# In the feed-forward part of a hybrid block: one sum of the down-projection on VectorE, the last pass's operands written by the up-projection, and the first two blocks' f read back

## The chip, the cores and the metric

The kernel runs on one core of a Trainium2 chip. The metric is the time of one execution in microseconds (us) of device time. PE is TensorE, DVE is VectorE, ACT is ScalarE, POOL is GpSimd, and SP is the engine that issues the DMAs.

## The reference

One layer over x of 2048 rows by 1024. Four mixers (a dilated attention, an RG-LRU, an SSD and a differential attention) read a projection of the normalised rows; their outputs are projected, normalised and added to x. Then comes the feed-forward part, which alone is touched here:

```
u = rms_norm(h, norm_ffn_pre)
f = square(relu(u @ w_ff_up))        # 2048 x 4096
h = h + rms_norm(f @ w_ff_down, norm_ffn_post)
```

## The kernel before

**Products.** Both projections are done by a scheme with seven products for a 2 by 2 block product in place of eight. Each number in a matmul is split into two float16 parts (a rounded one and a remainder), and each product takes three matmuls (`mm3`). A split is one ACT instruction (the rounded part) and one DVE instruction (the remainder). `TURN` is the order of the seven products: 0, 5, 6, 4, 1, 3, 2.

**Up-projection.** It has 32 blocks (g, cp): g = 0..15 is a pair of 128 columns of f, cp = 0, 1 a half of the rows. `up_block` runs the products into PSUM banks X, Y, Z, V, in the order X, Y, Z, V, X, Z, V. ACT applies relu and square into the two tiles `e` (f = 0 and 1), and `put` writes f to DRAM (`fD`). For all blocks but (0, 0) and (1, 0), `up_operands` makes the operands for j = 0 and 2 of the four j (128 rows each): four sums `fz` on POOL, seven splits `fs`, two writes to `fO`. `put` then writes only j = 1 and 3. The tiles of a block come from the pool `fuw` or, every other block, from `fst`; when the last of `fst` is released, the pools of the down-projection can open there.

**Down-projection.** It runs in six passes over g, in the order `QS` = 1, 2, 0, 3, 4, 5 (`PASSES`: passes 0 and 1 have two pairs g, the others three). A pass has eight blocks (cp, j), a block 42 matmuls in a pass of two pairs and 63 in one of three. `f_operands` gets a block's operands `fo`: for j = 0 and 2 one DMA from `fO`; for j = 1 and 3, and for all j of pass 0, cp 0, it reads f back (`fr`, one buffer) and makes them (four POOL sums `ft`, seven ACT and seven DVE instructions). `down_weights` does the same for the weights (`dr`, `ds`, `dw`), three pairs ahead.

`down_block` sums the products into y, which stays in SBUF: s = X copied by ACT (`ds`), s += Y on DVE; POOL adds s to y22, y21 and y12, in this order; DVE adds the later banks, y22 += Z first. In these names y11 and y12 are the two halves of one row tile of y and y21 and y22 those of another. The Z bank takes two products, 6 and 3, so product 3 waits until DVE has done y22 += Z, and that add waits for the add of s to y22. Three products (6 into Z, 4 into V, 1 into X) stand between the end of Y and the second use of Z. The first pass (1) has no add of s, and in the last pass (5) DVE does y12's. After each block of the last pass, `finish` normalises two row tiles on ACT, POOL (`fgp`, `ms_f`, `rs_f`) and DVE (`y<-y,rs_f,fh`) and writes them out.

**Order.** Every instruction goes through the class `Loom` (its helper at L562 records them, so all rows have that line). It lists the whole program's work and issues it by a greedy plan: each engine's queue is filled in the order in which the plan's costs make the pieces ready, with priorities by lane ("down" and "fin" 0, "fform", "fprep" and "uprep" 1, "up" 2). Each engine then runs its queue strictly in order.

Of the kernel before, what the change touches and what calls it, by code (L numbers as in the profile page):

```python
# [10 lines left out]
F32 = mybir.dt.float32  # L11
F16 = mybir.dt.float16
# [7 lines left out]
P = 128  # L20
# [14 lines left out]
QS = (1, 2, 0, 3, 4, 5)  # L35
# [1584 lines left out]
class Ffn:  # L1620
# [8 lines left out]
    def __init__(self, k, w_up, w_dn, post, gain, u, ev, out):  # L1629
# [8 lines left out]
        for q, (p0, p1) in enumerate(PASSES):  # L1638
            for cp in range(2):
                self.f[q, cp] = k.dram.tile([4, P, 2 * (p1 - p0), 2 * P], F32, tag=f"fD{q}{cp}", name=f"fD{q}{cp}")  # L1640
                self.o[q, cp] = k.dram.tile([2, P, p1 - p0, 7, 2, P], F16, tag=f"fO{q}{cp}", name=f"fO{q}{cp}")
        self.w, self.d, self.n, self.made = {}, {}, 0, 0
# [65 lines left out]
    def up_block(self, g, cp):  # L1708
# [15 lines left out]
        def act(src, f, ab):  # L1724
            d = e[f][:, :, ab, :]
            nc.scalar.activation(d, src.rearrange("p (j t) -> p j t", j=4), AF.Relu, scale=2.0 ** -24)
            nc.scalar.activation(d, d, AF.Square)

        def put(f):
            x = 2 * (g - PASSES[q][0]) + f  # L1730
            j = slice(1, 4, 2) if q + cp else slice(0, 4)
            nc.sync.dma_start(self.f[q, cp][j, :, x, :].rearrange("j p c -> p j c"),
                              e[f][:, j].rearrange("p j a t -> p j (a t)"))
        q = next(i for i, (p0, p1) in enumerate(PASSES) if p0 <= g < p1)
        with nc.lane("up", 2):
# [27 lines left out]
            act(add(V)[:], 0, 1)  # L1763
            put(0)
        if q + cp:
            self.up_operands(q, g - PASSES[q][0], cp, e)

    def up_operands(self, q, x, cp, e):

        k, nc = self.k, self.k.nc  # L1770
        with nc.lane("fform", 1, DVE=1.0):
            a = [e[f][:, 0:4:2, ab, :] for ab in range(2) for f in range(2)]
            z = [self.ev.tile([P, 512], F32, tag=f"at{i % 2}", name=f"fz{q}{x}{cp}{i}")[:, 0:256]
                 .rearrange("p (j t) -> p j t", j=2) for i in range(4)]
            sums(nc.gpsimd, *a, *z)
            src = dict(in_turn(*a, *z, False))
            for n in (0, 4):
                w = self.ev.tile([P, 2, 4, 2, P], F16, tag="e1", name=f"fs{q}{x}{cp}{n}")
                m = min(4, 7 - n)
                for i in range(m):  # L1780
                    split_to(nc, src[SHELF[n + i]], w[:, :, i, 0, :], w[:, :, i, 1, :])
                nc.sync.dma_start(self.o[q, cp][:, :, x, n:n + m].rearrange("j p i h t -> p j (i h t)"),
                                  w[:, :, 0:m].rearrange("p j i h t -> p j (i h t)"))
# [16 lines left out]
    def f_operands(self, q, cp, j):  # L1800
# [3 lines left out]
        with nc.lane("fprep", 1, DVE=1.0):  # L1804
            if q + cp and j % 2 == 0:
                w = k.fdr.tile([P, n, 7, 2, P], F16, tag="fo", name=f"fo{q}{cp}{j}", bufs=2)
                nc.sync.dma_start(w[:].rearrange("p n i h t -> p (n i h t)"),
                                  self.o[q, cp][j // 2].rearrange("p n i h t -> p (n i h t)"))
                return w
# [11 lines left out]
    def down_block(self, q, cp, j):  # L1821
# [17 lines left out]
        with nc.lane("down", 0):  # L1839
# [9 lines left out]
            if not first:  # L1849
                for o in (y22, y21, y12):  # L1850
                    (nc.gpsimd if not last or o is not y12 else nc.vector).tensor_tensor(o, o, s, op=ALU.add)
# [52 lines left out]
    def run(self):  # L1904
# [6 lines left out]
        for g, cp in blocks:  # L1911
            while ready < min(n, g + 2):
                self.up_weights(ready, 1)
                ready += 1
                for x in range(8) if ready == 2 else (ready + 5,) if 2 < ready < 11 else ():
                    self.down_top(x)
            self.up_block(g, cp)
        self.down_scale()
        self.y = [k.fd.tile([P, D], F32, tag=f"y{t}", name=f"y{t}") for t in range(NT)]
# [145 lines left out]
```

## Times and profile before

| | us |
|---|---|
| median of 3 runs (2623.23, 2630.83, 4965.94) | 2630.83 |
| the profiled execution | 2625.73 |
| its span | 2624.0 |
| PE busy / DVE / ACT / POOL | 2450.8 / 1843.2 / 1286.4 / 1157.3 |
| mean granted TensorE clock | 0.974 of full speed |

Times within the profile are from the span's start. The mixers, the output projection and the norm come before the up-projection's steady part. The down-projection's first matmul stands at 1960.82. Its first two passes (1 and 2) end near 2168, pass 0 fills 2168 to 2262, passes 3 and 4 run to about 2488, pass 5 ends at 2613, and 11 us of output follow.

### The profile page before, as it was taken

The numbers are of one execution on the slowest core, as the hardware profiler recorded it, in microseconds if no ns is written. First come the engines' busy times: TensorE is split into PE (matmuls) and PEld (weight loads), VectorE is DVE, ScalarE is ACT, GpSimd is POOL, SyncE is SP. The second block draws the span as 40 slices with busy tenths as digits, with TensorE's granted clock in tenths as the row PEclk, the third lists the DMA queues.
The fourth block names the chain that finished last, engine by engine and source line by source line (L and its number), as shares of the span: only waits on it lengthen the run. The fifth ranks groups of instructions, "written<-read, shape, count | busy, mean of one in ns | idle before, by whom it ended". The sixth has DMA issues, their size and how long they took to land.

```text
span 2624.0 us, 39878 instructions
## 1 busy us (share of the span) xinstructions
PE 2450.8 (93%) x14186; PEld 1297.1 (49%) x14186; DVE 1843.2 (70%) x3973; ACT 1286.4 (49%) x2705; POOL 1157.3 (44%) x1195
## 2 busy tenths in 40 slices
PE   7999999999999997997897999999998998999987
PEld 5555475666645555653444444444443443444433
DVE  6487986766788778757735776666648758747576
ACT  6377775433456667644435555555545323313222
POOL 5373331020266444534521444444325647747476
PEclk9999999999999998997998999999999999999998
DMA  6522226362351435236632443433334322323255
GB/s 189 151 71 85 84 71 191 66 179 56 79 149 56 123 108 161 86 90 204 197 113 78 143 148 132 145 103 107 117 118 161 126 71 87 118 96 113 78 174 163
DMA packets 277944, 313.90 MB, mean 120 GB/s; under 512 B 51381, under 2 KB 227957, under 8 KB 275184
## 3 DMA queue, kind: packets, MB, share of 16 engines
q1 hardware_dynamic: 277743, 311.35, 38.1%
q8 instruction: 112, 1.84, 0.3%
q14 instruction: 89, 0.72, 0.1%
HBM read 215.27 MB, written 102.83 MB: 121 GB/s over the span
## 4 chain that ended last, share of the span: by engine, by line
PE 60%; DVE 16%; POOL 7%; DMA 7%; issue 5%; ACT 3%; SPq 2%; DVEq 0%; POOLq 0%; ACTq 0%
PE mz L562 10%; PE mv L562 10%; PE mx L562 10%; PE my L562 5%; PE pt L562 5%; DVE e L562 3%; PE po L562 3%; PE as L562 2%; DVE fo L562 2%; PE pv L562 2%; PE do L562 2%; SPq L562 2%; PE dt L562 2%; POOL y L562 2%; DVE dw L562 1%
## 5 line engine op out<-in xcount | busy, mean ns | idle before, releaser
L562 PEld LDWEIGHTS <-fo 128*128 128x128 f16 x2688 | 264.9, 99 | 379.0 <-issue 63.6
L562 PEld LDWEIGHTS <-uw 128*128 128x128 f16 x2688 | 263.3, 98 | 311.7 <-issue 0.8
L562 PE MATMUL pt<-uuh,wl 128*128 128x512 f16 x640 | 243.9, 381 | 0.7 <-DVE wl L562 0.7
L562 PE MATMUL pt<-uuh,wh 128*128 128x512 f16 x640 | 244.3, 382 | 0.1
L562 PE MATMUL pt<-uul,wh 128*128 128x512 f16 x640 | 244.0, 381 | 0.0
L562 POOL TENSOR_TENSOR y<-y,ds 128x512 f32<-128x512 f32 x112 | 163.5, 1483 | 154.8 <-DVE ds L562 154.8
L562 DVE CUSTOM_DVE_ANT_0 e<-sc,strip,scf 128x512 f32<-128x512 f32 (+3 forms) x320 | 205.9, 663 | 25.3 <-PE sc L562 15.2
L562 PE MATMUL mz<-dw,fo 128*128 128x512 f16 x768 | 188.4, 389 | 34.0 <-DVE y L562 33.7
L562 ACT ACTIVATE e<-e,dmn 128x1024 f32<-128x1024 f32 (+4 forms) x192 | 171.4, 895 | 46.0 <-DVE dmn L562 43.4
L562 PE MATMUL mx<-dw,fo 128*128 128x512 f16 x768 | 183.4, 382 | 9.2 <-ACT ds L562 5.2
L562 PEld LDWEIGHTS <-wh 128*128 128x128 f16 x1280 | 123.2, 99 | 126.1 <-issue 22.3
L562 PE MATMUL mv<-dw,fo 128*128 128x512 f16 x768 | 184.4, 383 | 0.9 <-DVE y L562 0.9
L562 PE MATMUL po<-woh,mx 128*128 128x512 f16 x512 | 168.5, 393 | 10.6 <-ACT mx L562 6.3
L562 PE MATMUL mx<-u,uw 128*128 128x512 f16 x768 | 177.5, 380 | 0.0
L562 PE MATMUL mz<-u,uw 128*128 128x512 f16 x768 | 177.0, 379 | 0.0
L562 PE MATMUL mv<-u,uw 128*128 128x512 f16 x768 | 177.0, 379 | 0.0
L562 POOL TENSOR_SCALAR e<-e,dcf 128x256 f32<-128x256 f32 (+4 forms) x96 | 74.0, 770 | 160.9 <-DVE dcf L562 112.1
L562 ACT ACTIVATE ae<-ae,mt 128x256 f32<-128x256 f32 (+1 forms) x192 | 87.2, 455 | 114.3 <-DVE mt L562 100.2
L562 PEld LDWEIGHTS <-mx 128*128 128x128 f16 x768 | 76.6, 101 | 99.1 <-issue 9.5
L562 POOL TENSOR_TENSOR ur<-ur,g_ffn 128x1024 f32<-128x1024 f32 x32 | 61.3, 1922 | 134.4 <-DMA ur<-in_w_ff_up_dram 83.7
L562 PE MATMUL sc<-k,q 128*128 128x512 f16 (+3 forms) x320 | 102.4, 350 | 13.0 <-DVE dmn L562 9.3
L562 ACT ACTIVATE at<-dt 128x512 f32<-128x512 f32 (+3 forms) x160 | 80.7, 527 | 68.6 <-PE dt L562 64.4
(332 smaller groups left out, 5616.9 us busy)
## 6 DMA issues: line engine op xcount, KB each, us to landing
dr<-in_w_ff_down_dram SPq DMA_DIRECT2D x64, 512.0 KB, 3.7
fo<-fO SPq DMA_DIRECT2D x16, 1344.0 KB, 5.6
ur<-in_w_ff_up_dram SPq DMA_DIRECT2D x32, 512.0 KB, 5.2
fD<-e SPq DMA_DIRECT2D x60, 256.0 KB, 2.2
fO<-fs SPq DMA_DIRECT2D x30, 512.0 KB
wr<-in_w_in_dram SPq DMA_DIRECT2D x24, 512.0 KB
fr<-fD SPq DMA_DIRECT2D x16, 768.0 KB, 4.3
fO<-fs SPq DMA_DIRECT2D x30, 384.0 KB, 3.7
```

The costliest lines, as they stand in the source:

```text
L562: op.ins.append(fn(*[real(a) for a in args], **{n: real(a) for n, a in kw.items()}))
```

## The change

Four edits go together.

1. `down_block`: y22 += s is a DVE instruction in all passes that have it (5 passes of 8 blocks, 40 instructions from POOL to DVE). POOL keeps y21 and y12, and y21 alone in the last pass.
2. For the last pass (q = 5, g = 13 to 15) `up_operands` makes the operands of all four j: `fz` 512 columns wide in place of 256, the splits too, in four tiles of two operands in place of two of four (24 writes to `fO` in place of 12). `put` writes no f there. `f_operands` loads all eight `fo` of that pass; the four reads `fr` and the 4 x (4 POOL, 7 ACT, 7 DVE) instructions of blocks j = 1 and 3 are gone.
3. After the 5th and the 7th up-projection block (those are (2, 0) and (3, 0)), f of blocks (0, 0) and (1, 0) is read back from DRAM into tiles of `fuw` (`eb00`, `eb01`, `eb10`, `eb11`, 256 KB each), and `up_operands` makes their operands for j = 0 and 2: 2 x (4 POOL, 7 ACT, 7 DVE). In pass 0 the blocks (0, 0) and (0, 2) then load `fo`, and as many instructions are gone there.
4. `act` claims both tiles `e` of a block at its first write.

PE's instructions are the same in number. Up to the 5th block of the up-projection, at about 1478 us, the order on all engines is that of before.

```diff
@@ class Ffn, __init__
-                self.o[q, cp] = k.dram.tile([2, P, p1 - p0, 7, 2, P], F16, tag=f"fO{q}{cp}", name=f"fO{q}{cp}")
+                self.o[q, cp] = k.dram.tile([4, P, p1 - p0, 7, 2, P], F16, tag=f"fO{q}{cp}", name=f"fO{q}{cp}")
...
@@ up_block
             d = e[f][:, :, ab, :]
+            nc.claim(e[0], e[1])
...
-            nc.sync.dma_start(self.f[q, cp][j, :, x, :].rearrange("j p c -> p j c"),
-                              e[f][:, j].rearrange("p j a t -> p j (a t)"))
+            if q != QS[-1]:
+                nc.sync.dma_start(self.f[q, cp][j, :, x, :].rearrange("j p c -> p j c"),
+                                  e[f][:, j].rearrange("p j a t -> p j (a t)"))
...
+        self.made_last = e
         if q + cp:
             self.up_operands(q, g - PASSES[q][0], cp, e)
@@ up_operands
         with nc.lane("fform", 1, DVE=1.0):
-            a = [e[f][:, 0:4:2, ab, :] for ab in range(2) for f in range(2)]
-            z = [self.ev.tile([P, 512], F32, tag=f"at{i % 2}", name=f"fz{q}{x}{cp}{i}")[:, 0:256]
-                 .rearrange("p (j t) -> p j t", j=2) for i in range(4)]
+            js = slice(0, 4, 1 if q == QS[-1] else 2)
+            nj, ni = (4, 2) if q == QS[-1] else (2, 4)
+            if e is None:
+                e = [k.fuw.tile([P, 4, 2, P], F32, tag="er", name=f"eb{x}{f}", bufs=2) for f in range(2)]
+                nc.claim(*e)
+                nc.need(*self.made_last.values())
+                for f in range(2):
+                    nc.sync.dma_start(e[f][:, js].rearrange("p j a t -> p j (a t)"),
+                                      self.f[q, cp][js, :, 2 * x + f, :].rearrange("j p c -> p j c"))
+            a = [e[f][:, js, ab, :] for ab in range(2) for f in range(2)]
+            z = [self.ev.tile([P, 512], F32, tag=f"at{i % 2}", name=f"fz{q}{x}{cp}{i}")[:, 0:nj * P]
+                 .rearrange("p (j t) -> p j t", j=nj) for i in range(4)]
             sums(nc.gpsimd, *a, *z)
             src = dict(in_turn(*a, *z, False))
-            for n in (0, 4):
-                w = self.ev.tile([P, 2, 4, 2, P], F16, tag="e1", name=f"fs{q}{x}{cp}{n}")
-                m = min(4, 7 - n)
+            for n in range(0, 7, ni):
+                w = self.ev.tile([P, nj, ni, 2, P], F16, tag="e1", name=f"fs{q}{x}{cp}{n}")
+                m = min(ni, 7 - n)
...
@@ f_operands
-            if q + cp and j % 2 == 0:
+            if j % 2 == 0 or q == QS[-1]:
...
@@ down_block
             if not first:
-                for o in (y22, y21, y12):
+                add(y22, y22, s)
+                for o in (y21, y12):
                     (nc.gpsimd if not last or o is not y12 else nc.vector).tensor_tensor(o, o, s, op=ALU.add)
@@ run
             self.up_block(g, cp)
+            if self.made in (5, 7):
+                self.up_operands(0, (self.made - 5) // 2, 0, None)
```

The plan lays the queues out anew from these edits. Three places show it. The first is ACT in the up-projection, at the block after the first read-back: `e21...` are the f tiles of block (2, 1), `fs10..` the split operands of block (1, 1), `fs00..` those of the block read back, `uw4_...` the seven weight operands of g = 4. Before:

```order
L562 ACTIVATE fs1004_16754<-fz1000_16708 128x2x128
L562 ACTIVATE fs1004_16754<-fz1001_16729 128x2x128
L562 ACTIVATE fs1004_16754<-fz1002_16737 128x2x128
L562 ACTIVATE e211_16770<-c21_16735 128x4x128
L562 ACTIVATE e211_16770<-e211_16770 128x4x128
L562 ACTIVATE e210_16792<-mx_16669 128x4x128
```

After the change:

```order
L562 ACTIVATE fs0004_16835<-fz0002_16815 128x2x128
L562 ACTIVATE uw4_0_16844<-ur40_16655,s_up4_16827 128x512
L562 ACTIVATE uw4_5_16847<-us41_16768,s_up4_16827 128x512
L562 ACTIVATE uw4_6_16853<-us42_16785,s_up4_16827 128x512
L562 ACTIVATE uw4_4_16856<-us40_16752,s_up4_16827 128x512
L562 ACTIVATE uw4_1_16860<-ur40_16655,s_up4_16827 128x512
L562 ACTIVATE uw4_3_16863<-ur41_16667,s_up4_16827 128x512
L562 ACTIVATE uw4_2_16866<-us43_16803,s_up4_16827 128x512
L562 ACTIVATE e211_16869<-c21_16739 128x4x128
L562 ACTIVATE e211_16869<-e211_16869 128x4x128
L562 ACTIVATE e210_16870<-mx_16669 128x4x128
L562 ACTIVATE e210_16870<-e210_16870 128x4x128
```

Ahead of this piece stand the four rounded parts `fs0000` and the first two of `fs0004`. So the seven splits of the block read back and the seven of g = 4's weights now stand between `fs1004` and `e210<-mx`, the instruction that frees bank X; before, the weights' stood behind it. On POOL the order there is `us42`, `fz0000`, `us43`, `fz0001`, `fz0002`, `fz0003`.

The second place is DVE in pass 0, block (0, 3), where `ds003` is s, y7 holds y22 and y21, y3 holds y11 and y12, and `dw9_...` are weight splits for g = 9. Before:

```order
L562 TENSOR_TENSOR ds003_22944<-ds003_22944,my_22959 128x512
L562 SCALAR_TENSOR_TENSOR dw9_6_22966<-ds92_22949,kd_14614,dw9_6_22966 128x512
L562 SCALAR_TENSOR_TENSOR dw9_4_22973<-ds90_22845,kd_14614,dw9_4_22973 128x512
L562 SCALAR_TENSOR_TENSOR dw9_1_22976<-dr91_22884,kd_14614,dw9_1_22976 128x512
L562 TENSOR_TENSOR y7_21345<-y7_21345,mz_22927 128x512
```

After the change:

```order
L562 SCALAR_TENSOR_TENSOR dw9_4_22989<-ds90_22877,kd_14614,dw9_4_22989 128x512
L562 TENSOR_TENSOR ds003_23003<-ds003_23003,my_22999 128x512
L562 TENSOR_TENSOR y7_21411<-y7_21411,ds003_23003 128x512
L562 TENSOR_TENSOR y7_21411<-y7_21411,mz_22982 128x512
L562 SCALAR_TENSOR_TENSOR dw9_1_22997<-dr91_22892,kd_14614,dw9_1_22997 128x512
```

The weight splits that stood between s and y22 += Z stand ahead of s or behind the add.

The third place is DVE in the last pass, block (0, 2): y6 holds y22 and y21, y2 holds y11 and y12, and y5 is a row tile that is being finished. Before, block (0, 0), where `fo501` is the next block's operands:

```order
L562 TENSOR_TENSOR ds500_25004<-ds500_25004,my_24999 128x512
L562 TENSOR_TENSOR fo501_24986<-fr501_24825,fo501_24986 128x3x128
L562 TENSOR_TENSOR y0_21256<-y0_21256,ds500_25004 128x512
L562 TENSOR_TENSOR fo501_24986<-ft501_24876,fo501_24986 128x3x128
L562 TENSOR_TENSOR y4_21267<-y4_21267,mz_24981 128x512
```

After the change, block (0, 2), which is the pattern of the later blocks:

```order
L562 TENSOR_TENSOR ds502_25209<-ds502_25209,my_25205 128x512
L562 SCALAR_TENSOR_TENSOR y5_21299<-y5_21299,rs_f5_25214,fh5_25133 128x1024
L562 TENSOR_TENSOR y6_21420<-y6_21420,ds502_25209 128x512
L562 TENSOR_TENSOR y2_21419<-y2_21419,ds502_25209 128x512
L562 TENSOR_TENSOR y6_21420<-y6_21420,mz_25186 128x512
```

No split of `fo` is left in the pass; a step of `finish` and the two adds of s stand between s and y22 += Z. At the passage to the down-projection, POOL's order was `fz5200`, `ds42`, `fz5201`, `fz5202`, `fz5203`, `ds43` and is now `ds42`, `fz5200`, `ds43`, `fz5201`, `fz5202`, `fz5203`, with `fz` twice as wide.

## Rows read from the trace of the kernel before

**Rows 1.** Windows: start:end, us, busy (x) by engine, PEclk, DMA share, GB/s.

```profile
1450.00:1955.00 505.00, 505.00 (x2354) 231.61 (x2353) 324.64 (x582) 282.07 (x537) 202.67 (x194) 1.00 0.36 121
1955.00:2002.00 47.00, 36.53 (x159) 15.48 (x158) 38.92 (x61) 27.36 (x58) 23.65 (x23) 0.96 0.55 190
2002.00:2168.00 166.00, 165.00 (x764) 74.50 (x762) 115.95 (x168) 55.66 (x112) 93.11 (x76) 1.00 0.32 108
2168.00:2262.00 94.00, 78.05 (x333) 33.31 (x332) 76.70 (x100) 28.71 (x61) 67.90 (x56) 0.95 0.31 99
2262.00:2502.00 240.00, 233.69 (x1075) 105.36 (x1073) 146.30 (x203) 60.23 (x115) 137.59 (x108) 0.99 0.29 100
2502.00:2613.00 111.00, 97.08 (x428) 42.26 (x426) 86.28 (x84) 27.90 (x56) 80.67 (x78) 0.97 0.56 173
```

**Rows 2.** Waits 1930 to 2624: who waited for whom, us, times, longest.

```profile
PE mz L562 <- DVE y L562: 33.7, 15, 4.0
DVE y L562 <- POOL y L562: 21.4, 16, 1.8
```

**Rows 3.** PE timeline, passes 0, 4, 5: start, us, instruction, [idle before <-releaser].

```profile
2213.30 1.97 PE L562 MATMUL mz<-dw,fo 128*128 128x512 f16 x6 [3.86 <-DVE y L562]
2411.76 3.72 PE L562 MATMUL mz<-dw,fo 128*128 128x512 f16 x9 [4.00 <-DVE y L562]
2540.89 2.10 PE L562 MATMUL mz<-dw,fo 128*128 128x512 f16 x9
2558.95 3.73 PE L562 MATMUL mz<-dw,fo 128*128 128x512 f16 x9 [3.92 <-DVE y L562]
```

**Rows 4.** DVE timeline, pass 0, block (0, 3).

```profile
2207.98 0.67 DVE L562 TENSOR_TENSOR ds<-ds,my 128x512 f32<-128x512 f32 x1
2208.58 2.41 DVE L562 SCALAR_TENSOR_TENSOR dw<-ds,kd,dw 128x512 f16<-128x512 f32 x2
...
2212.57 0.68 DVE L562 TENSOR_TENSOR y<-y,mz 128x512 f32<-128x512 f32 x1
```

**Rows 5.** POOL timeline, pass 0 block (0, 3) and pass 4.

```profile
2208.73 5.05 POOL L562 TENSOR_TENSOR y<-y,ds 128x512 f32<-128x512 f32 x3 [1.96 <-DVE ds L562]
2405.96 4.59 POOL L562 TENSOR_TENSOR y<-y,ds 128x512 f32<-128x512 f32 x3 [2.50 <-DVE ds L562]
```

**Rows 6.** Groups of tile y, 1990 to 2613: duration min/median/max ns, first, last start.

```profile
L562 POOL TENSOR_TENSOR y<-y,ds x112: 1255/1444/2925, 2061.1 to 2607.6; 128x512 f32<-128x512 f32 x112
L562 DVE SCALAR_TENSOR_TENSOR y<-y,rs_f,fh x14: 1271/1540/3354, 2503.7 to 2608.1; 128x1024 f32<-128x1024 f32 x14
```

**Rows 7.** DVE and POOL timelines of the last pass, two blocks.

```profile
2535.21 2.59 DVE L562 TENSOR_TENSOR y<-y,ds 128x512 f32<-128x512 f32 x1
2534.90 2.35 POOL L562 TENSOR_TENSOR y<-y,fgp 128x1024 f32<-128x1024 f32 x1
2601.72 0.69 DVE L562 TENSOR_TENSOR y<-y,ds 128x512 f32<-128x512 f32 x1
```

**Rows 8.** ACT, POOL and PE timelines of the up-projection, 1481 to 1500.

```profile
1484.82 1.34 ACT L562 ACTIVATE fs<-fz 128x256 f16<-128x256 f32 x4 [5.31 <-POOL fz L562]
1489.28 0.60 ACT L562 ACTIVATE e<-mx 128x512 f32<-128x512 f32 x1 [0.58 <-PE mx L562]
1495.15 1.93 ACT L562 ACTIVATE uw<-us,s_up 128x512 f16<-128x512 f32 x3
1488.81 1.45 POOL L562 TENSOR_TENSOR us<-ur,us 128x512 f32<-128x512 f32 x1
1494.48 2.75 PE L562 MATMUL mx<-u,uw 128*128 128x512 f16 x12
```

**Rows 9.** POOL, ACT and PE timelines at the passage to the down-projection.

```profile
1985.88 0.72 POOL L562 TENSOR_TENSOR fz<-e,fz 128x256 f32<-128x256 f32 x1
1988.36 0.58 ACT L562 ACTIVATE ds<-mx 128x512 f32<-128x512 f32 x1
1988.99 2.72 PE L562 MATMUL mx<-dw,fo 128*128 128x512 f16 x6 [5.24 <-ACT ds L562]
```

More of the change, by code (lines that the diff above doesn't have):

```diff
@@ L1771, in up_operands @@
         with nc.lane("fform", 1, DVE=1.0):
-            a = [e[f][:, 0:4:2, ab, :] for ab in range(2) for f in range(2)]
-            z = [self.ev.tile([P, 512], F32, tag=f"at{i % 2}", name=f"fz{q}{x}{cp}{i}")[:, 0:256]
-                 .rearrange("p (j t) -> p j t", j=2) for i in range(4)]
+            js = slice(0, 4, 1 if q == QS[-1] else 2)
[10 more added lines that the diff above has]
+                 .rearrange("p (j t) -> p j t", j=nj) for i in range(4)]
             sums(nc.gpsimd, *a, *z)
             src = dict(in_turn(*a, *z, False))
-            for n in (0, 4):
-                w = self.ev.tile([P, 2, 4, 2, P], F16, tag="e1", name=f"fs{q}{x}{cp}{n}")
-                m = min(4, 7 - n)
+            for n in range(0, 7, ni):
+                w = self.ev.tile([P, nj, ni, 2, P], F16, tag="e1", name=f"fs{q}{x}{cp}{n}")
+                m = min(ni, 7 - n)
                 for i in range(m):
                     split_to(nc, src[SHELF[n + i]], w[:, :, i, 0, :], w[:, :, i, 1, :])
-                nc.sync.dma_start(self.o[q, cp][:, :, x, n:n + m].rearrange("j p i h t -> p j (i h t)"),
+                nc.sync.dma_start(self.o[q, cp][js, :, x, n:n + m].rearrange("j p i h t -> p j (i h t)"),
                                   w[:, :, 0:m].rearrange("p j i h t -> p j (i h t)"))
@@ L1804, in f_operands @@
         with nc.lane("fprep", 1, DVE=1.0):
-            if q + cp and j % 2 == 0:
+            if j % 2 == 0 or q == QS[-1]:
                 w = k.fdr.tile([P, n, 7, 2, P], F16, tag="fo", name=f"fo{q}{cp}{j}", bufs=2)
                 nc.sync.dma_start(w[:].rearrange("p n i h t -> p (n i h t)"),
-                                  self.o[q, cp][j // 2].rearrange("p n i h t -> p (n i h t)"))
+                                  self.o[q, cp][j].rearrange("p n i h t -> p (n i h t)"))
                 return w
```

## The prediction

> **What bounds the kernel now.** I read the windows by stage first [rows 1], because an average over the span would mix stages with different limits. In the up-projection (1450 to 1955) TensorE is busy 505.00 of 505 us: nothing that another engine saves there can be worth anything, and anything that makes TensorE wait there costs its full length. The window 2002 to 2168 (passes 1 and 2) gives the pitch of a matmul: 165.00 us / 764 = 0.216 us. By that pitch the other windows lose
>
> - 1955 to 2002: 47 - 159 x 0.216 = 12.7 us,
> - 2168 to 2262 (pass 0): 94 - 333 x 0.216 = 22.1 us,
> - 2262 to 2502 (passes 3 and 4): 240 - 1075 x 0.216 = 7.8 us,
> - 2502 to 2613 (pass 5): 111 - 428 x 0.216 = 18.6 us.
>
> So the down-projection from pass 0 on loses 48.5 us in all, part of it idle and part of it at a lower granted clock (0.95 to 0.99).
>
> Next, who is waited for [rows 2]: TensorE's product into Z waits 33.7 us, 15 times, for a DVE add into y, and DVE's y in turn 21.4 us for POOL's y. The timeline of PE shows such stalls of about 4 us [rows 3]; the matmuls behind one run slower (nine in 3.73 us where nine take 2.10), so a stall of 4.0 us costs about 1.6 us more.
>
> What holds that add up is seen in one block of pass 0 [rows 4, 5]. s is ready at 2208.65. DVE then splits weights (two in 2.41 us, more behind them), while POOL adds s to y22, y21 and y12, three in 5.05 us. y22 += Z starts only at 2212.57, and TensorE goes on at 2213.30 [rows 3]. From the end of product Y, three products stand ahead of the one that needs Z free: 3 x 6 x 0.216 = 3.9 us in a pass of two pairs, 3 x 9 x 0.216 = 5.8 us in one of three. That is the due time which decides.
>
> **The change part by part.**
>
> *y22 += s on DVE.* Forty instructions leave POOL, whose three take 4.59 to 5.05 us in these rows [rows 5] (median 1.44 each [rows 6]), and DVE gets forty of 0.69 us where POOL leaves it alone, 2.59 us where not [rows 7]. The path is now s 0.67, y22 += s 0.69, y22 += Z 0.68: 2.0 us after Y, if nothing stands between. The order shows nothing between them in the block whose rows I read; where operands are split, one or two splits stay between, and two splits beside POOL take 2.41 us [rows 4], so 4.5 us against 3.9.
>
> - Pass 0: I allow 0.6 us for six of its eight blocks, 3.6 us. It gives back 22.1 - 3.6 = 18.5 us. That two of its blocks load `fo` and split nothing is in this sum. Ends: 8 us (the splits of all blocks stay ahead and POOL holds them) and 22.
> - Passes 3 and 4: the due time is 5.8 us, so 2.0 plus two splits fits. I leave 1.3 us: gain 6.5 us (ends 3 and 7.8).
>
> *Last pass.* Its splits leave POOL, ACT and DVE altogether, and that work is hidden except on DVE's way to y22 += Z. But two other things stand there now: a step of `finish` (1.27 us at the least, 1.54 median, 3.35 at the most [rows 6]) and both adds of s. Cheapest: 0.67 + 1.27 + 0.69 + 0.69 + 0.68 = 4.0 us, no stall. Dearest: 0.67 + 3.35 + 2.59 + 2.59 + 0.68 = 9.9 us, a stall of 4.1 us in every block. With the median step and one of the adds held by POOL: 0.67 + 1.54 + 2.59 + 0.69 + 0.68 = 6.2 us, 0.4 us late; I take 0.8 us per block for the differences between blocks, 6.6 us in all. Gain 18.6 - 6.6 = 12 us (ends 4 and 18). The four `fo` loads more replace four `fr` reads; the DMA share of the window is 0.56 [rows 1], and a load has a whole block of 63 x 0.216 = 13.6 us to land: nothing.
>
> *The read-back in the up-projection.* Its DMAs and POOL sums stand beside other work, yet ACT's queue does not absorb it. Before, ACT frees bank X with `e<-mx` at 1489.28 to 1489.88, and TensorE needs X at 1494.48 [rows 8]: 4.6 us to spare. Now the seven splits of the block read back and the seven of g = 4 stand ahead of it. POOL's `us43` ended at 1488.81 + 1.45 = 1490.3; the four `fz` are added ahead of the moment when the first tile can be finished, 4 x 0.72 us [rows 9], so 1493.1. From there ACT does four splits (4 x 1.34 / 4 = 1.3 us), seven weight splits (7 x 1.93 / 3 = 4.5 us) and three instructions of 0.6 us: bank X is free at 1500.7, and TensorE has waited 1500.7 - 1494.5 = 6.2 us. With the slower matmuls behind such a stall (1.6 us), 7.8 us. Since nothing waits for anything but TensorE here, all of it reaches the end. Ends: 0 (POOL takes `fz` so early that ACT is through in the 5.31 us which it now idles ahead of its splits [rows 8]) and 15 (the second read-back stalls as well). At the second, POOL's four sums stand together and the last weight splits behind `e<-mx`; what is added ahead of it is the seven splits, 7 x 0.34 = 2.3 us of a slack like the 4.6 us, so I cost it at nothing; if that slack is gone, it costs as much as the first.
>
> *Wider operands at the end of the up-projection.* `fz` over 512 columns takes POOL 1.26 us (its shortest add of that width [rows 6]) in place of 0.72 [rows 9]. For block (15, 1): 4 x 0.54 = 2.2 us later release of the tile on which the pools of the down-projection wait, so 2.2 us later loads. For block (15, 0): 2.2 us again, a `ds` of 1.26 us that is now ahead of the last three sums, and four wider ACT splits, 4 x (0.64 - 0.34) = 1.2 us [rows 8]. Behind these splits stands ACT's `ds<-mx` at 1988.36, and for it TensorE already waits 5.24 us [rows 9]. So the sum goes straight onto that wait: 2.2 + 2.2 + 1.3 + 1.2 = 6.9 us. Ends: 2.2 (only the loads) and 10. The earlier blocks of g = 13 to 15 have the 2.2 us more on POOL inside a slack like those 4.6 us and are costed at nothing.
>
> *Sum*: -18.5 - 6.5 - 12 + 7.8 + 6.9 = -22.3 us. The profiled execution took 2625.7 us; it lies between the two lower of the runs shown (2623.2 and 2630.8, the latter the median). So **2603.4, forecast 2604 us**.
>
> **A rule against the change.** Each moved add reads two tiles in SBUF, and the rows show what POOL does to it: started 0.31 us behind a POOL instruction of 2.35 us it took 2.59 us, and alone 0.69 us [rows 7]. The Trainium skill's page "SBUF — State Buffer", section "Who interferes with whom", states this as an exclusive lock: a VectorE instruction with two SBUF inputs contends with a GpSimd instruction that reads SBUF, and the second to issue blocks fully. By that rule the trace agrees, and moving an add between these two engines frees neither. If all forty moved adds took 2.59 us, the path in passes of two pairs would be 0.67 + 2.59 + 0.68 = 3.9 us, just the due time, and in those of three pairs within 5.8 us. So I keep the gain for passes 0, 3 and 4; the place where the lock decides is the last pass, which makes the fourth rival.
>
> **The rivals.**
>
> 1. *As summed*, 2604 us: chance 0.50.
> 2. *The adds come in order behind splits and steps of `finish`.* TensorE goes on waiting for the same add, now behind DVE's own queue. For it: one or two splits between s and y22 += Z in four blocks of pass 0, a step of `finish` in seven of the last pass. Against: the due times. Gains of 9, 5 and 8 in place of 37 in all: -22 + 14.7 = -7, so 2618 us. Chance 0.22.
> 3. *The costs are hidden.* The read-back's splits and the wider ones find room: for it ACT's idle 5.31 us; against it TensorE's 505.00 of 505, which leaves no room behind a stall. -37 + 2 gives 2591 us. Chance 0.16.
> 4. *Slower: the last pass locks.* Three two-input instructions stand in a row on DVE ahead of y22 += Z while POOL runs its normalising products of 2.35 us. If each of the three is held as in the dearest case, seven blocks stall 4.1 us and pay 1.6 us of clock: 40 us in place of 18.6, +21. With pass 0, 3 and 4 as summed: +21 - 25 + 14.7 = +11, so 2637 us. It decides from the point where y22 += Z ends more than 5.8 us behind Y. For it: 2.59 and 3.35 us occur. Against: they do not occur together in the rows, and POOL has four `ft` sums per odd block less. Chance 0.09.
> 5. That the change does not do what it says: the order has the forty adds on DVE, no split in the last pass, and the loads. No chance; what is left (0.03) is for a second stall in the up-projection beside the first, at about 2612 us.
>
> **How the numbers follow.** The likeliest case's own range is 2594 to 2614. The range for 8 in 10 takes in most of case 3 and case 2 with 6 us of difference between runs: 2589 to 2624. Case 4 and the best of case 3 are left out. Two per cent is 53 us, and about what a measurement of this kernel tells from no change: below 2578 us no case lies but the sum of all the upper ends (0.02), above 2683 us none but a disturbed measurement or several stalls at once (0.01). Within: 0.97.
>
> **What would show it.** Right: window of pass 0 down from 94 to about 76 us; the wait of PE's `mz` for DVE's y down from 33.7 to about 10 us; a stall of PE's `mx` of about 6 us near 1494 with ACT's `e` named; the wait for ACT's `ds` after the up-projection up from 5.2 us to about 10. Wrong: no stall near 1494 (rival 3), DVE rows `y<-y,ds` of more than 2 us in the last pass with `mz` stalls of 4 us behind them (rival 4), or splits standing between `ds` and `y<-y,mz` where PE waits (rival 2).

## The result, and the profile after

The changed kernel takes 2610.08 us (median of 6 runs, 2604.17 to 3146.88) against 2631.1 for the kernel before (6 runs). The ratio is 0.9923 with a 95% interval of 0.9903 to 0.9942, so some 20 us less; the forecast was 2604 us in a range of 2589 to 2624. The comparison leaves disturbed runs, such as the longest ones here, out; without them these medians are 2609.07 and 2630.83 us, and that of the add alone, in the table of experiments, is 2605.31 in place of 2607.08. The profiled execution took 2611.13 us (span 2609.4), 14.6 us less than the one before; between two profiled executions the unchanged part ahead of the feed-forward part alone differs by several us (the last transposes of its norm start between 1416.6 and 1429.0 in the kernels told of below), so stages are compared below by what TensorE loses in each.

Four windows of the changed kernel, with the columns of [rows 1] and cut at about the same places of the program: the up-projection, pass 0, passes 3 and 4, and the last pass.

```profile
1450.00:1955.00 505.00, 499.35 (x2326) 228.75 (x2324) 340.30 (x590) 286.60 (x542) 217.63 (x198) 1.00 0.39 130
2183.00:2260.00 77.00, 70.97 (x323) 31.42 (x322) 69.38 (x95) 23.58 (x48) 55.35 (x42) 1.00 0.36 123
2260.00:2500.00 240.00, 237.32 (x1091) 106.98 (x1090) 164.10 (x218) 60.39 (x114) 116.22 (x87) 0.99 0.29 102
2500.00:2599.00 99.00, 92.63 (x424) 41.26 (x422) 71.45 (x70) 20.09 (x36) 62.19 (x62) 1.00 0.69 216
```

The first window is no longer full: TensorE idles 5.65 us of 505. Pass 0's window fell from 94 to 77 us (some 2 us of that because it holds 323 matmuls where it held 333), the last pass's from 111 to 99. The waits from 1930 on, as in [rows 2]; the line of DVE's y for POOL's y, 21.4 us before, is not there any more:

```profile
PE mz L562 <- DVE y L562: 14.0, 17, 2.2
PE mx L562 <- ACT ds L562: 9.9, 1, 9.9
```

Its PE timeline at the stalls, which answers to [rows 3] and to the PE rows of [rows 8, 9]:

```profile
1502.87 2.75 PE L562 MATMUL mz<-u,uw 128*128 128x512 f16 x12 [1.91 <-ACT e L562]
1512.83 2.75 PE L562 MATMUL mz<-u,uw 128*128 128x512 f16 x12 [2.03 <-DVE c L562]
...
1970.02 1.46 PE L562 MATMUL mx<-dw,fo 128*128 128x512 f16 x3 [2.88 <-DMA fo<-fO]
...
2003.62 2.72 PE L562 MATMUL mx<-dw,fo 128*128 128x512 f16 x6 [9.88 <-ACT ds L562]
...
2217.40 1.46 PE L562 MATMUL mz<-dw,fo 128*128 128x512 f16 x6 [1.26 <-DVE y L562]
...
2229.14 1.45 PE L562 MATMUL mz<-dw,fo 128*128 128x512 f16 x6 [1.64 <-DVE y L562]
...
2550.30 2.10 PE L562 MATMUL mz<-dw,fo 128*128 128x512 f16 x9 [0.82 <-DVE y L562]
```

Stalls of up to 4 us for DVE's y in the down-projection have become stalls of at most 2.2 us; new ones stand in the up-projection, and the one at the passage has grown from 5.24 to 9.88 us.

In the table, a stage's loss is the sum, over the rows of PE's timeline, of the time to the next row's start less the number of matmuls times 0.216 us, where that is over 0.15 us (so idle time and slower matmuls together). The passage is the stretch from the first down-projection matmul to some 25 us behind the last of the up-projection.

| loss, us | before | after | after - before | forecast |
|---|---|---|---|---|
| up-projection | 0.0 | 6.3 | +6.3 | +7.8 |
| passage | 12.9 | 20.0 | +7.1 | +6.9 |
| passes 1 and 2, rest | 1.5 | 2.7 | +1.2 | 0 |
| pass 0 | 21.8 | 7.3 | -14.5 | -18.5 |
| passes 3 and 4 | 8.4 | 4.8 | -3.6 | -6.5 |
| pass 5 | 18.4 | 6.6 | -11.8 | -12 |
| sum | 63.0 | 47.7 | -15.3 | -22.3 |

### The profile page after: what moved, and what is told of

Its sections match the earlier page's. It is cut to its first block, busy times and chain, and to the rows that moved or that the text cites. A ratio compares the mean times of both kernels' runs of the same rounds, so it can differ in the third digit from the quotient of the medians.

```text
span 2609.4 us, 39806 instructions
## 1 busy us (share of the span) xinstructions
PE 2445.9 (94%) x14186; PEld 1296.0 (50%) x14186; DVE 1868.3 (72%) x3985; ACT 1283.8 (49%) x2677; POOL 1111.3 (43%) x1139
## 4 chain that ended last, share of the span: by engine, by line
PE 61%; DVE 16%; DMA 8%; POOL 6%; issue 5%; ACT 3%; SPq 2%; DVEq 0%; POOLq 0%; ACTq 0%
PE mz L562 10%; PE mv L562 10%; PE mx L562 10%; PE my L562 5%; PE pt L562 5%; PE po L562 4%; DVE e L562 3%; DVE y L562 2%; PE as L562 2%; PE pv L562 2%; PE do L562 2%; PE dt L562 2%; SPq L562 2%; PE ao L562 1%; PE atp L562 1%
## 5 line engine op out<-in xcount | busy, mean ns | idle before, releaser
L562 PE MATMUL mx<-dw,fo 128*128 128x512 f16 x768 | 183.7, 382 | 14.6 <-ACT ds L562 9.9
L562 PE MATMUL mz<-dw,fo 128*128 128x512 f16 x768 | 182.8, 381 | 14.0 <-DVE y L562 14.0
L562 POOL TENSOR_TENSOR y<-y,ds 128x512 f32<-128x512 f32 x72 | 113.7, 1596 | 156.9 <-DVE ds L562 156.9
```

What stands on the lines that cost most here:

```text
L562: op.ins.append(fn(*[real(a) for a in args], **{n: real(a) for n, a in kw.items()}))
```

## The experiments

**The parts alone.** The first kernel has the first edit alone:

```diff
-                for o in (y22, y21, y12):
+                add(y22, y22, s)
+                for o in (y21, y12):
```

> Only the first edit: y22 += s on DVE in all passes, nothing else. Theory (each edit acts in its own stage): passes 0, 3 and 4 get nearly what they got in the whole change (pass 0 there -14.7 us, passes 3 and 4 -3.5), the up-projection and its end are as before, and the last pass, with its splits still on DVE, gains a few us: 2608 to 2614 us against 2626, the stalls of the product into Z behind DVE's y down from 33.7 to about 16 us. Rival (pass 0 gains because two of its blocks load their operands and split nothing): pass 0 still loses over 14 of its 22 us, and the whole is above 2616.

The second has the second edit alone: `up_operands` for four j where q == QS[-1], no f written there, all eight `fo` of pass 5 loaded.

> Only the last pass's operands made in the up-projection; all adds of s but y12's in the last pass stay on POOL, nothing is read back. Theory: the end of the up-projection loses the 7 us that it lost in the whole change (wait for ACT's ds near 10 us), pass 5 gains 8 to 12 us, the other passes are as before: 2620 to 2626 us. Rival (the last pass gains because of the add on DVE, not because of its splits): pass 5 still loses over 14 us, and the whole is at 2630 or more.

The third has the read-back and the claim alone:

```diff
+            nc.claim(e[0], e[1])
...
-            if q + cp and j % 2 == 0:
+            if j % 2 == 0:
...
+            if self.made in (5, 7):
+                self.up_operands(0, (self.made - 5) // 2, 0, None)
```

> Only f of the first two blocks read back and their operands made in the up-projection (with the claim of both tiles). Theory: the up-projection loses 5 to 6 us in stalls as in the whole change, pass 0 gains 2 to 6 us of its 22 since two of its blocks split nothing: 2624 to 2630 us, no gain. Rival (pass 0's gain comes from here): pass 0 gains over 8 us, 2618 to 2623.

The fourth is the whole change less the read-back:

```diff
-            if j % 2 == 0 or q == QS[-1]:
+            if q + cp and j % 2 == 0 or q == QS[-1]:
...
-            if self.made in (5, 7):
-                self.up_operands(0, (self.made - 5) // 2, 0, None)
```

> The whole change without the read-back (the first blocks' operands are made in pass 0 as before). Theory: the 5 to 6 us of stalls in the up-projection are gone, pass 0 loses 2 to 6 us more than in the whole change: 2606 to 2611 us, about as the whole change. Rival: pass 0 falls back by 8 us or more, 2614 or more.

Measured, with the losses by stage as in the table above (us; the ratio of the whole change is that of the result, against its own six runs of the kernel before):

| | median | ratio to before (95%) | up | passage | 1, 2 | 0 | 3, 4 | 5 | sum |
|---|---|---|---|---|---|---|---|---|---|
| before | 2627.3 | | 0.0 | 12.9 | 1.5 | 21.8 | 8.4 | 18.4 | 63.0 |
| add alone | 2607.08 | 0.9922 (0.9902 to 0.9943) | 0.0 | 13.4 | 1.1 | 12.5 | 4.6 | 14.4 | 46.0 |
| last pass alone | 2624.52 | 0.9995 (0.9984 to 1.0006) | 4.3 | 19.4 | 2.9 | 23.0 | 8.6 | 5.9 | 64.0 |
| read-back alone | 2627.76 | 1.0003 (0.9989 to 1.0017) | 5.2 | 15.1 | 0.2 | 17.7 | 9.2 | 19.7 | 67.2 |
| no read-back | 2606.7 | 0.9929 (0.991 to 0.9948) | 1.3 | 18.8 | 4.0 | 12.3 | 4.5 | 6.6 | 47.4 |
| whole change | 2610.08 | 0.9923 (0.9903 to 0.9942) | 6.3 | 20.0 | 2.7 | 7.3 | 4.8 | 6.6 | 47.7 |

The theory held in its main point, that each edit acts in its own stage, and in three of four totals (the add alone came out 1 us better than its 2608); its sizes did not all hold. Pass 0 gave the add alone 9 us and not "nearly" 14.5, the waits for DVE's y fell to 21.1 us there and not to 16, and the last pass alone lost 4.3 us in the up-projection that its theory did not have. The rivals fell in all four: with the add alone pass 0 lost 12.5 us and not over 14, and without the read-back it fell back by 5 us and not by 8. What the prediction had not expected stands in the ratios: **the one line gives the whole gain**, and the other two edits give back what they cost. The last pass's operands save 12.5 us in pass 5 (18.4 to 5.9) and cost 6.5 us at the passage and 4.3 in the up-projection; the read-back saves 4 to 5 us in pass 0 and costs 5 in the up-projection.

**How the one line acts.** The prediction read [rows 2] as one chain: TensorE waits for y22 += Z, and that add for POOL's y22 += s. For most of the stalls the rows show something else. Of TensorE's 15 waits before the change (33.7 us), only four, 4.4 us together, stand behind an add for which DVE had waited for POOL; none of TensorE's waits follows the other twelve of DVE's 16 waits for POOL. In the remaining eleven, 29.3 us, DVE had no gap: between s and y22 += Z it worked through splits, and in the last pass through y12's add and a step of `finish` too. In the block of [rows 4] a third split, 1.74 us from 2210.91 on, stands ahead of the add. Another such block is (0, 0) of pass 0, before the change, DVE and then POOL:

```profile
2168.11 0.68 DVE L562 TENSOR_TENSOR ds<-ds,my 128x512 f32<-128x512 f32 x1
2168.71 0.41 DVE L562 TENSOR_TENSOR fo<-ft,fo 128x256 f16<-128x256 f32 x1
2169.04 2.89 DVE L562 TENSOR_TENSOR fo<-fr,fo 128x256 f16<-128x256 f32 x2
2171.86 1.48 DVE L562 TENSOR_TENSOR fo<-ft,fo 128x256 f16<-128x256 f32 x1
2173.26 0.67 DVE L562 TENSOR_TENSOR y<-y,mz 128x512 f32<-128x512 f32 x1
```

```profile
2168.86 4.19 POOL L562 TENSOR_TENSOR y<-y,ds 128x512 f32<-128x512 f32 x3 [2.23 <-DVE ds L562]
```

Beside POOL's adds the last three splits take 1.4 to 1.5 us each, where the first takes 0.41. The first of POOL's three adds, y22's, was done by about 2170.3 (an estimate: a third of 4.19 us), 3 us before y22 += Z started. The same block in the kernel with the add alone:

```profile
2166.31 0.68 DVE L562 TENSOR_TENSOR ds<-ds,my 128x512 f32<-128x512 f32 x1
2166.91 0.41 DVE L562 TENSOR_TENSOR fo<-ft,fo 128x256 f16<-128x256 f32 x1
2167.24 0.68 DVE L562 TENSOR_TENSOR y<-y,ds 128x512 f32<-128x512 f32 x1
2167.85 0.41 DVE L562 TENSOR_TENSOR fo<-fr,fo 128x256 f16<-128x256 f32 x1
2168.18 0.68 DVE L562 TENSOR_TENSOR y<-y,mz 128x512 f32<-128x512 f32 x1
```

Two splits stand between s and y22 += Z in place of four, none is slowed, and TensorE waits 0.71 us here where it waited 3.01. So the line acts at least in part through the order: with y22 += s in DVE's own queue, the plan puts y22 += Z close behind it and the splits elsewhere. A rival follows from this that no run tested, the add left on POOL and the splits planned behind y22 += Z. How much of the 20 us is due to the engine and how much to the order stays open.

**The last pass.** What still holds pass 5 when its operand work is gone is seen in the kernel with the second edit alone, DVE and then POOL at one block (columns as in [rows 4, 5]):

```profile
2547.81 2.93 DVE L562 SCALAR_TENSOR_TENSOR y<-y,rs_f,fh 128x1024 f32<-128x1024 f32 x1
...
2552.51 0.69 DVE L562 TENSOR_TENSOR y<-y,mz 128x512 f32<-128x512 f32 x1 [1.16 <-POOL y L562]
```

```profile
2551.13 1.35 POOL L562 TENSOR_TENSOR y<-y,ds 128x512 f32<-128x512 f32 x1
...
2552.58 1.26 POOL L562 TENSOR_TENSOR y<-y,ds 128x512 f32<-128x512 f32 x1
```

POOL's y22 += s still releases DVE here, and TensorE still loses only 0.9 us a block. Moving that add brings nothing more once that work is gone (5.9 us against 6.6 in pass 5). The other way round, the add alone leaves pass 5 at 14.4 us although no split stands between s and y22 += Z there any more: the step of `finish` takes up to 3.35 us and in three blocks starts only after a wait of 1.23 to 1.25 us for POOL. Which part of the work that the second edit removes (on POOL, ACT or DVE) had delayed that step was not taken apart.

In the whole change a block of pass 5 reads so on DVE, with POOL's normalising product beside it (second fence):

```profile
2543.76 0.69 DVE L562 TENSOR_TENSOR ds<-ds,my 128x512 f32<-128x512 f32 x1 [3.27 <-PE my L562]
2544.36 3.01 DVE L562 SCALAR_TENSOR_TENSOR y<-y,rs_f,fh 128x1024 f32<-128x1024 f32 x1
2547.30 2.35 DVE L562 TENSOR_TENSOR y<-y,ds 128x512 f32<-128x512 f32 x2
2549.57 0.68 DVE L562 TENSOR_TENSOR y<-y,mz 128x512 f32<-128x512 f32 x1
```

```profile
2543.93 2.36 POOL L562 TENSOR_TENSOR y<-y,fgp 128x1024 f32<-128x1024 f32 x1
...
2547.75 1.35 POOL L562 TENSOR_TENSOR y<-y,ds 128x512 f32<-128x512 f32 x1
```

The step of `finish` takes 3.01 us beside POOL where others take 1.28, and the add ends at 2550.25, when TensorE has been waiting 0.8 us. The next kernel plans that step later:

```diff
-        with nc.lane("fin", 0):
+        with nc.lane("fin", 0, DVE=3.0):
```

> The whole change, with the DVE step of finish planned 3 us later, so that it stands behind y22 += Z in the last pass. Theory: the 0.8 us by which each of seven blocks of pass 5 is late comes from that step (3.01 us beside POOL), so these stalls go, with about 1 us left of 6.6: 25 to 27 us below the kernel before, where the whole change is 20 below. Rival (the two adds of s alone, held by POOL, are late): the stalls stay above 0.5 us per block, 20 to 22 below.

Measured: median 2606.57, ratio 0.9915 (0.9891 to 0.994). Pass 5 loses 0.0 us, as expected; the rest is as in the whole change (43.8 us in all). The profile's line of PE's waits for DVE's y, 5.4 us in pass 5 of the whole change, is gone from that stretch, while the two adds of s still take 2.34 us together. So the step of `finish` was the cause, not the adds. The gain of 22 us against before lies at the rival's end of the total; by the profile the theory holds, and the total's interval is wider than the difference.

**The passage.** The long wait there follows the last block's operands on POOL, then ACT (whole change):

```profile
1999.11 1.27 POOL L562 TENSOR_TENSOR fz<-e,fz 128x512 f32<-128x512 f32 x1
```

```profile
2000.41 2.19 ACT L562 ACTIVATE fs<-fz 128x512 f16<-128x512 f32 x4 [7.91 <-POOL fz L562]
...
2002.98 0.58 ACT L562 ACTIVATE ds<-mx 128x512 f32<-128x512 f32 x1
```

Two kernels take the sums `fz` from POOL to DVE, first for both blocks of g = 15, then for (15, 0) alone (there on the change without the read-back and with `finish` later):

```diff
-            sums(nc.gpsimd, *a, *z)
+            sums(nc.vector if (q, x) == (5, 2) else nc.gpsimd, *a, *z)
```

> The whole change, with the four wide sums fz of the two blocks of g = 15 on DVE in place of POOL. Theory (POOL's wide sums hold the tiles on which the down-projection's pools wait): the wait for ACT's ds falls from 9.9 us to 5 or 6, the wait for the first fo from 2.9 to under 1; the passage loses 13 to 15 us in place of 20: 25 to 27 us below the kernel before. Rival (ACT's wider splits or the loads set it): the wait for ds stays above 8.5 us, 19 to 21 below.

Measured: median 2615.45, ratio 0.9946 (0.9927 to 0.9965). The wait for `ds` fell to 5.5 us, as expected, and that for the first `fo` to 1.3 (under 1 was expected), but the passage lost 23.9 us: other waits came. ACT first, then PE:

```profile
1973.93 0.63 ACT L562 ACTIVATE fs<-fz 128x512 f16<-128x512 f32 x1 [4.79 <-DMA fO<-fs]
```

```profile
1977.73 0.59 PE L562 MATMUL mx<-dw,fo 128*128 128x512 f16 x1 [4.29 <-ACT dw L562]
...
2007.53 2.72 PE L562 MATMUL mx<-dw,fo 128*128 128x512 f16 x6 [5.50 <-ACT ds L562]
```

The second edit writes four tiles `fs` per block where there were two. Once the sums are early, ACT's last split waits 4.79 us for the write to DRAM of an earlier tile, and the weight splits behind it in ACT's queue, which TensorE needs, wait with it. (Whether two tiles would have spared that wait was not tried.)

> The whole change without the read-back, with the step of finish planned later, and the four wide sums of the very last block of the up-projection, (15, 0), alone on DVE. Theory (POOL's queue holds the last sums, and in the run with both blocks' sums on DVE the new waits came from block (15, 1)'s): the wait for ACT's ds is 5 to 6 us in place of 9.9 and no new wait over 2 us comes in; pass 5 loses about 0; the whole is 28 to 34 us below the kernel before. Rival (DVE's sums delay whatever stands behind them in either block): new waits of 4 us or more at the passage, 22 to 26 below.

Measured: median 2600.95, ratio 0.9907 (0.9891 to 0.9924); losses 1.3, 18.6, 2.5, 11.9, 3.0, 0.0, in all 37.3 us, the least of all kernels here. Two waits of the run with both blocks' sums on DVE, 4.29 us for ACT's `dw` and 2.88 us for DVE's `c`, are gone, so block (15, 1)'s early sums had brought them; one of 2.47 us for `fo` (2.82 in that run) is there, and the wait for `ds` fell only to 8.66 us. DVE, then ACT and PE:

```profile
1984.29 0.69 DVE L562 TENSOR_TENSOR fz<-e,e 128x512 f32<-128x512 f32 x1 [1.36 <-ACT e L562]
1985.02 1.64 DVE L562 TENSOR_TENSOR fz<-fz,e 128x512 f32<-128x512 f32 x1
...
1988.25 1.78 DVE L562 TENSOR_TENSOR fz<-e,fz 128x512 f32<-128x512 f32 x1
```

```profile
1994.40 0.63 ACT L562 ACTIVATE fs<-fz 128x512 f16<-128x512 f32 x1 [2.66 <-DMA fO<-fs]
```

```profile
1996.05 2.72 PE L562 MATMUL mx<-dw,fo 128*128 128x512 f16 x6 [8.66 <-ACT ds L562]
```

The first sum takes 0.69 us; while POOL sums weights from 1984.52 on, the next three take 1.64 to 1.78. Then ACT waits again for a write. So neither held as written: no new wait of 4 us, but 25 us below before and not 28. DVE's four sums took 5.7 us beside POOL's work, and without ACT's wait of 2.66 us the wait for `ds` would have been 6.0 (an estimate: 8.66 less 2.66). This version is below both kernels in median, by 0.9% against the one before; against the changed one the intervals overlap.

Of the next three, the first and the last change the plan alone: the order of the queues, not what an instruction waits for on the chip. The second puts changes together.

**POOL's adds behind DVE's.**

```diff
                 for o in (y21, y12):
+                    if not last:
+                        nc.need(y[tb])
```

> The whole change, with POOL's adds of s to y21 and y12 made to start only after DVE's y22 += s (not in the last pass). Theory (POOL's adds hold DVE's): y22 += s falls from a median of 1.24 us to about 0.7, and pass 0 loses 3 to 5 us in place of 7.4: 23 to 25 us below the kernel before. Rival (splits in DVE's own queue ahead of the add decide): the add gets shorter, but pass 0 still loses over 6 us, 19 to 22 below.

Measured: median 2611.26, ratio 0.9923 (0.9902 to 0.9944); pass 0 lost 9.1 us. The median of y22 += s on DVE fell to 0.87 us, but in the block with the longest stall POOL's adds still started 0.18 us ahead of it, and it took 1.75: the plan's dependence does not bind the engines. So it does not tell what POOL's adds cost, and that stays open.

**Three together**: this one, `finish` later and both blocks' sums on DVE, on the change without the read-back.

> The whole change without the read-back, with all three: the step of finish later, the sums of g = 15 on DVE, POOL's adds behind DVE's. Theory: the parts add up, -20 for the change as it is, -6 for finish, -6 for the passage, -3 for POOL: about 35 us below the kernel before, near 2592. Rival (what one stall gives back, the next takes, since the plan is laid anew): under 28 us below.

Measured: median 2608.23, ratio 0.9921 (0.9904 to 0.9939); losses 1.4, 23.8, 2.0, 13.0, 4.6, 0.0. The rival held. Against the change without the read-back (12.3 in pass 0, 18.8 at the passage), of the 6.6 us won in pass 5, 5.0 were lost at the passage and 0.7 in pass 0.

**Splits planned later.** In pass 0 of the whole change, DVE at block (0, 3) (compare [rows 4]):

```profile
2212.12 2.62 DVE L562 SCALAR_TENSOR_TENSOR dw<-ds,kd,dw 128x512 f16<-128x512 f32 x2 [0.24 <-ACT dw L562]
2214.66 0.67 DVE L562 TENSOR_TENSOR ds<-ds,my 128x512 f32<-128x512 f32 x1
2215.37 1.19 DVE L562 TENSOR_TENSOR y<-y,ds 128x512 f32<-128x512 f32 x1
2216.66 0.69 DVE L562 TENSOR_TENSOR y<-y,mz 128x512 f32<-128x512 f32 x1
```

Now the splits stand ahead of s and make s itself late. So:

```diff
-        with nc.lane("fprep", 1, DVE=1.0):
+        with nc.lane("fprep", 1, DVE=4.0):
...
-        with nc.lane("dprep", prio, DVE=1.0):
+        with nc.lane("dprep", prio, DVE=4.0):
```

> The whole change, with the DVE parts of the operand and weight splits in the down-projection planned 4 us later, so that in pass 0 no split stands between s and y22 += Z, and fewer ahead of s. Theory (what passes 0, 3 and 4 still lose, 7.4 and 4.9 us, is DVE's own queue: splits ahead of s and of the add): pass 0 loses 2 to 4 us and passes 3 and 4 together under 2.5; 25 to 28 us below the kernel before. Rival (POOL's lock on the adds is what is left): pass 0 still loses over 6 us; or the later splits come too late for TensorE and appear as waits for dw or fo.

Measured: median 2612.31, ratio 0.9946 (0.9926 to 0.9966). Passes 3 and 4 lost 0.6 us: there the queue of splits was the cause. Pass 0 still lost 8.5, part of it a new wait of 1.8 us for `fo`; at the passage the wait for `ds` fell to 6.0 us, but waits of 3.4 us for DVE's `dw` and 2.6 for `fo` took its place, so that passage and passes 1 and 2 together lost 23.2 us where the whole change lost 22.7. That is the rival's second half. In pass 0 the splits now stand behind y22 += Z but ahead of the next add, the one out of V, for which TensorE waits 1.16 us twice; so the cause of what pass 0 loses is not settled by this run.

**The first edit with the plan changed**, `finish` later and, from pass 0 on, the operand splits 4 us later:

> Only the first edit, y22 += s on DVE, with two changes of the plan: the DVE step of finish 3 us later, and from pass 0 on the DVE parts of the operand splits 4 us later, so that hardly any split stands between s and y22 += Z. No wide operands, no read-back. Theory (the path s, y22 += s, y22 += Z is what counts, and the other two edits only pay for themselves): the passage loses 13 us as before the change, pass 0 5 to 7, passes 3 and 4 under 2, pass 5 under 3: 35 to 42 us below the kernel before, 2585 to 2592. Rival (the last pass needs its splits gone, and splits planned later come too late for TensorE): pass 5 loses over 8 us or waits for fo appear; under 25 below.

Measured: median 2613.86, ratio 0.994 (0.9923 to 0.9958); losses 0.0, 12.9, 1.4, 17.4, 7.6, 6.1. The rival held. One row of PE shows why:

```profile
2206.23 3.03 PE L562 MATMUL mx<-dw,fo 128*128 128x512 f16 x7 [5.85 <-DVE fo L562]
```

The split that was moved out of the add's way came 5.85 us too late for the next block: on DVE it ran at 2205.23, behind weight splits, although ACT's half of it was done at 2199.7.

**The same plan on the change without the read-back:**

> The same two changes of the plan on the whole change without the read-back: the last pass's operands come from the up-projection. Theory: the passage loses 20 us, 7 more than without the wide operands, and pass 5 gains 1 to 3 us less than that: 28 to 36 us below the kernel before, 4 to 7 us behind the run with the first edit alone and the same plan. Rival (with splits out of the last pass it is the better one): ahead of that run.

Measured: median 2608.69, ratio 0.9924 (0.9909 to 0.9939); losses 1.4, 19.3, 4.4, 16.9, 7.5, 0.0. The 28 us of the theory were missed by 9. Its median is ahead of the run with the first edit alone, which loses 6.1 us in pass 5; but the intervals overlap, and by the losses it is behind (49.5 us in all against 45.4), so which of the two is better is not shown.

## Why the prediction was right

**The forecast** held: 2610 us in 2589 to 2624, and the direction. In part that is luck. By the losses the change is worth 15.3 us and by the profiled executions 14.6, where the sum had 22.3; the medians differ by 21 us in part because the one of before lies 5 us above the execution from which the forecast was counted. And the mechanism was read rightly only down to y22 += Z. TensorE's second product into Z did wait for that add, and with y22 += s on DVE no wait of DVE for POOL's y is left; but 29.3 of the 33.7 us of stalls stood behind splits in DVE's own queue and not behind POOL's y22 += s. That these splits leave the gap was seen in the order of the queues, and the gain is there for that reason at least in part. Five of the steps, by their own terms:

- *Pass 5*, 12 us forecast, 11.8 measured, and 0.8 us per block as forecast. But where the sum had 0.67 + 1.54 + 2.59 + 0.69 + 0.68 the rows show 0.69 + 3.01 + 2.35 + 0.68: beside POOL it is the step of `finish` that is long, rather than one add. The moved add has no part in this gain, since without it (the last pass alone) pass 5 loses 5.9 us.
- *Passage*, 6.9 us forecast, 7.1 measured, on the wait that was named: `ds` 4.64 us longer (5.24 to 9.88) where 4.7 of the sum were for it. For the loads the sum had 2.2 us and their wait grew by 1.1 (1.75 to 2.88); 1.6 us of slower matmuls behind that wait, which were not in the sum, make up for it.
- *Read-back*, 7.8 us forecast, 4.9 measured in three stalls (1.91, 2.03 and 0.46 us idle); the rest of the 6.3 is a wait of 1.24 us for the scale of the down weights at 1908, which only kernels with the wider operands have. ACT's rows there, to set beside those of [rows 8]:

```profile
1495.53 1.33 ACT L562 ACTIVATE fs<-fz 128x256 f16<-128x256 f32 x4 [6.95 <-POOL fz L562]
...
1502.24 0.58 ACT L562 ACTIVATE e<-mx 128x512 f32<-128x512 f32 x1
```

  The bank was free at 1502.8, close to the 1500.7 worked out (the block as a whole runs 1.1 us later in this execution); the due time was wrong. TensorE needed that bank not for the next X at 1494.48 but for the Z after it, two products of 2.59 us later, as the row at 1502.87 says (`mz`, not `mx`). And the splits made DVE late as well (the stall at 1512.83), which I had not costed.
- *Pass 0*, 18.5 us forecast, 14.5 measured; *passes 3 and 4*, 6.5 and 3.6. **This is the term that was mis-sized**: I left 3.6 us to pass 0 (0.6 us for six blocks) and 1.3 us to passes 3 and 4. Pass 0 lost 7.3, in six blocks of 0.3 to 2.3 us, and passes 3 and 4 lost 4.8. Together 6.9 of the 7 us by which the sum is off; the other differences cancel. Two things lengthen the path of 2.0 us from Y.

  The first is a late s. At block (0, 3) TensorE was due at 2217.40 - 1.26 = 2216.14, so Y had ended 3.9 us earlier, at 2212.2; but s += Y started at 2214.66, behind the weight splits of the row at 2212.12, so the path began 2.4 us late. ACT's copy of X, to which Y is added, was itself behind weight splits in ACT's queue and ended only 1.6 us after Y:

```profile
2213.22 0.57 ACT L562 ACTIVATE ds<-mx 128x512 f32<-128x512 f32 x1
```

  In passes 3 and 4, one block (TensorE's stall of 2.25 us at 2409.01) makes 4.1 of the 4.8 us; its s += Y starts 3.2 us after Y.

  The second is POOL's two adds of s. The sum took 0.69 us for DVE's add in passes 0, 3 and 4, and the case of a held add was reckoned only with nothing else between the adds. In block (1, 0), DVE and then POOL:

```profile
2224.40 0.67 DVE L562 TENSOR_TENSOR ds<-ds,my 128x512 f32<-128x512 f32 x1
...
2225.33 1.75 DVE L562 TENSOR_TENSOR y<-y,ds 128x512 f32<-128x512 f32 x1
2227.01 1.48 DVE L562 TENSOR_TENSOR fo<-fr,fo 128x256 f16<-128x256 f32 x1
2228.41 0.67 DVE L562 TENSOR_TENSOR y<-y,mz 128x512 f32<-128x512 f32 x1
```

```profile
2225.15 3.05 POOL L562 TENSOR_TENSOR y<-y,ds 128x512 f32<-128x512 f32 x2 [3.42 <-DVE ds L562]
```

  These are the five instructions of the add-alone block shown above. There they took 2.55 us and in block (0, 2) of this kernel 2.54; here, and in blocks (0, 0) and (1, 2), they take 4.7, since the add and the split behind it are each 1.07 us longer. The three blocks lose 4.1 of pass 0's 7.3 us. By these rows (an estimate) none of the three would stall without the 2.1 us, nor, to within 0.1 us, without the split between the adds.

**The rivals.** The second, adds in order behind splits and steps of `finish`, is true in part: for passes 3 and 4, where splits planned later took the loss to 0.6 us, and for pass 0 as just read; it also describes most of the stalls before the change. The third fell with the stall at 1502.87 and the 9.88 us. The fourth did not occur: in the last pass the adds take 2.35 us for two beside POOL, not 2.59 each, and the stalls are 0.8 us, not 4.1. The rule of the Trainium skill, page "SBUF — State Buffer", section "Who interferes with whom", is that a VectorE instruction with two SBUF inputs contends with a GpSimd instruction that reads SBUF. This trace bears it out too: DVE's adds of s (forty of y22, eight of y12) take 0.677 us at the least and 1.238 in the median, and the median of POOL's own adds of s is 1.71 us where it was 1.44:

```profile
L562 POOL TENSOR_TENSOR y<-y,ds x72: 1258/1706/2589, 2076.1 to 2591.5; 128x512 f32<-128x512 f32 x72
L562 DVE TENSOR_TENSOR y<-y,ds x48: 677/1238/1758, 2076.4 to 2591.6; 128x512 f32<-128x512 f32 x48
```

By itself it did not decide: with the longest of these adds, 1.758 us, the path 0.67 + 1.76 + 0.69 = 3.1 us still fits the due time of 3.9. With a split between the adds that is slowed too, or with a late s, it does not fit.

What stays open: whether the gain needs the add on the other engine or only the other order of DVE's queue; what pass 0 would lose with POOL's two adds out of the way (the rows above give an estimate, no run shows it); and why the scale at 1908 comes later with the wider operands.

## What to carry to other kernels

When TensorE waits for a chain of small adds, look at each stall for what the last add stood behind: another engine's add, or other work in its own engine's queue. A wait between two engines in the list of waits need not be the one that holds TensorE. Here one line, which put the first add beside the next on one engine, gave all of the 20 us, though most of the stall was splits that the plan had put between them. Work that is moved from a late stage to an early one has to pass the early stage's own due times; where that stage is full (505.00 of 505 us), price every instruction that is queued ahead of one that frees a bank. And try the parts of a change alone: two of these three, as they were planned here, only paid for themselves.

## What the runs showed that I had not expected

- With four split tiles per block in place of two, ACT waited 2.66 to 4.79 us for a write to DRAM as soon as the sums ahead of them were early; with late sums the rows show no such wait. That the number of tiles is the cause is not shown.
- DVE sums of 128x512 from SBUF took 0.69 us alone and 1.64 to 1.78 us in a row beside POOL's sums: longer than on POOL itself, where one took 1.27.
- The wait for X's bank fell on Z: the next product to use a bank is not always the one of the same name.
